# A SwiGLU down projection: where the third tile's sums are loaded, when the last norm's vectors are loaded, and the order of the weight loads

## The chip, the cores and the metric

The kernel runs on one core of a Trainium2 chip. The metric is the device time of one execution, in microseconds; lower is better. A change counts as faster or slower here from two per cent on.

## What is computed

One decoder block over 256 tokens of width 1024: two token mixers with a shared input projection, an output projection, a layer norm, and a SwiGLU feed-forward layer with 2816 hidden features and a second layer norm. The change is in the last lines, the down projection and the norm behind it:

```python
D_MODEL = 1024
SEQ = 256
D_FF = 2816

def layer_norm(x, w, b):
    mu = jnp.mean(xf, axis=-1, keepdims=True)
    var = jnp.mean(jnp.square(xf - mu), axis=-1, keepdims=True)
    y = (xf - mu) * lax.rsqrt(var + LN_EPS) * w + b
    ...

    x = layer_norm(DN_ALPHA * x + mixed, ln1_w, ln1_b)
    h = jnp.einsum('bsd,df->bsf', x, w_ffn_in)
    h_gate, h_up = jnp.split(h, 2, axis=-1)
    y = jnp.einsum('bsf,fd->bsd', jax.nn.silu(h_gate) * h_up, w_ffn_down)
    return layer_norm(DN_ALPHA * x + y, ln2_w, ln2_b)
```

## The kernel before

**Precision.** Every float32 operand is split in two float32r parts: ScalarE casts it to the high part, VectorE subtracts to get the low part. TensorE then makes three products for one (high by high, high by low, low by high). A weight tile therefore goes through a load, a cast on ScalarE and a subtraction on VectorE before TensorE can use it.

**The down projection.** The 2816 rows of the down weights are 11 tiles of 256 rows by 1024 columns. Eight of them are *fast* tiles: their 2 x 2 blocks are multiplied by a Strassen-Winograd scheme with seven block products instead of eight, so 21 matmuls of 512 columns a tile. Three of the weight blocks are blocks of the tile itself (the *corners*), four are sums of blocks (the *sums*). The activations' sums are made when the hidden features come out (lines 1017 to 1022). The other three tiles are *plain* (`rows_pass`). `SEQUENCE` takes the fast tiles first, then the plain ones. In the built program the weights are numbered through the whole kernel: the fast tiles are 66 (first) to 73 (eighth), so 68 is the third and 69 the fourth, and the plain ones are 74 to 76.

**Where the sums come from.** `DOWN = "STTSTTSTPPP"` says it by tile. In an S tile (first, fourth, seventh) VectorE makes the sums from the corners' raw weights, in two places of 1024 columns, `cst` and `mv1` (lines 246 to 250); in a T tile (second, third, fifth, sixth, eighth) they were made much earlier, during the up projection, by DMAs that add in DRAM (`sum_weights`), and are loaded from there like a weight (line 271).

**Places.** Raw weights are loaded into `wraw` (3 places of 1 MB, one place is freed by the subtraction on VectorE of the tile that holds it) or into `big` (12 places of 1 MB, which activations, the residual and the norms' vectors use as well). `whi` and `wlo`, 4 places each, hold the high and low parts; a place is free again when TensorE has made its last product with it. Before the change the corners of the fourth to eighth tile go to `big` (line 254) and all loaded sums to `wraw`. The last norm's vectors `wb2`, 2 x 512 KB broadcast over the partitions by GpSimd's queue, take a place of `big` ahead of the down projection (line 1030).

**Order.** PE, DVE and Activation run in the order of the code in this part (`manual_schedule`). SyncE's loads are put in order by the scheduler. A queue is in order: a load whose place is not free holds those behind it.

Of the kernel before, what the change touches and what calls it, by code (L numbers as in the profile page):

```python
# [10 lines left out]
F32 = mybir.dt.float32  # L11
# [6 lines left out]
P = 128  # L18
T = 256
NT = T // P  # L20
D = 1024
# [24 lines left out]
FAST = tuple(range(2, 2 + len(DOWN) - DOWN.count("P")))  # L46
PLAIN = tuple(q for q in range(NF // 2) if q not in FAST)
SEQUENCE = [PLAIN[DOWN[:i].count("P")] if s == "P" else FAST[i - DOWN[:i].count("P")] for i, s in enumerate(DOWN)]
SUMMED = [q for q, s in zip(SEQUENCE, DOWN) if s == "T"]

C_ID = 0
# [32 lines left out]
def plan():  # L84
# [3 lines left out]
    def add(w, k0, kn, c0, n, held=False):  # L88
        tiles.append((w, k0, kn, c0 if isinstance(c0, tuple) else (c0,), n, held))
# [29 lines left out]
    for j in range(EARLY, NF, 2):  # L119
        add("w_ffn_in", 0, 8, j * P, 256)  # L120
        add("w_ffn_in", 0, 8, FF + j * P, 256)
    for q in SEQUENCE:
        add("w_ffn_down", 2 * q, 2, 0, 1024)
# [4 lines left out]
def hybrid_layer_kernel(ctx: ExitStack, tc, x, xw, vecs, bias, wts, ln1_w, ln1_b, ln2_w, ln2_b, consts, out):  # L128
    nc = tc.nc
    pool = lambda name, bufs, **kw: ctx.enter_context(tc.tile_pool(name=name, bufs=bufs, **kw))  # L130
    cp = pool("cp", 1)
# [9 lines left out]
    def slot(name, dt=F32):  # L141
        return big.tile([P, 2048], dt, tag="s8", name=name)

    def r32(ap):
        return ap.bitcast(F32)
# [32 lines left out]
    down = {t[1] // 2: i for i, t in enumerate(tiles) if t[0] == "w_ffn_down"}  # L178
# [6 lines left out]
    corners = {}  # L185
    dram = pool("dram", 1, space=bass.MemoryType.DRAM)
    summed = {down[q]: dram.tile([P, 2048], F32, tag=f"sums{q}", name=f"sums{q}") for q in SUMMED}
    state = {"next": 0}
# [9 lines left out]
    def stage(pieces=None, eng=nc.vector):  # L198
# [18 lines left out]
        for ks in ks_of(pieces or (k,)):  # L217
            nc.sync.dma_start(raw[:, ks, :], src[:, ks, :])
            if i in SUMS_AFTER and ks.start == 0:
                sum_weights(down[SUMMED[SUMS_AFTER.index(i)]])  # L220
            nc.scalar.copy(h[:, ks, :], raw[:, ks, :])  # L221
# [5 lines left out]
    quarters = lambda z: z.rearrange("p (b c) -> p b c", b=4)  # L227
# [13 lines left out]
    def stage_fast(i, kind):  # L241


        def make_sums(b):
            y, z = corners[i] = [v.rearrange("p (b c) -> p b c", b=2) for v in (
                cst, cp.tile([P, D], F32, tag="mv1", name=f"sums{i}"))]
            nc.vector.tensor_add(y, b[:, 1:3, :], b[:, 0:1, :].to_broadcast([P, 2, 512]))
            yield
            nc.vector.tensor_add(z[:, 0, :], b[:, 2, :], y[:, 0, :])
            nc.vector.tensor_add(z[:, 1, :], b[:, 3, :], z[:, 0, :])  # L250

        beside = kind == "corners" and i not in [down[q] for q in SEQUENCE[0:3]]
        raw = lambda: quarters(slot(f"raw{kind}{i}") if beside else
                               wraw.tile([P, 2048], F32, tag="raw", name=f"raw{kind}{i}"))
        h = quarters(whi.tile([P, 2048], F32R, tag="h", name=f"wh{kind}{i}"))
        l = quarters(wlo.tile([P, 2048], F32R, tag="l", name=f"wl{kind}{i}"))
        if kind == "corners":
            b = raw()
            n = 1 if i in summed else 0
            nc.sync.dma_start(b[:, n:4, :], quarters(wts[i])[:, n:4, :])  # L260
            sums = make_sums(b) if n == 0 else iter(())
            next(sums, None)
            h, l = h[:, 0:3, :], l[:, 0:3, :]
            nc.scalar.copy(h, b[:, 1:4, :])  # L264
            yield
            list(sums)
            nc.vector.tensor_sub(l, b[:, 1:4, :], r32(h))  # L267
            yield
        elif i in summed:
            z = raw()  # L270
            nc.sync.dma_start(z, quarters(summed[i]))
            nc.scalar.copy(h, z)  # L272
            yield
            nc.vector.tensor_sub(l, z, r32(h))  # L274
            yield
        else:
            for z, bs in zip(corners.pop(i), (slice(0, 2), slice(2, 4))):
                nc.scalar.copy(h[:, bs, :], z)
                yield
                nc.vector.tensor_sub(l[:, bs, :], z, r32(h[:, bs, :]))  # L280
                yield
        ready.append((h, l))
# [14 lines left out]
    cst = cp.tile([P, C_MASK], F32, tag="cst", name="cst")  # L297
# [165 lines left out]
    for j in range(4):  # L463
        sg = sm.tile([P, 2, T], F32, tag="sg", name=f"sgq{j}")
        sgs = [by_half(sg[:, f, :]) for f in range(2)]
        if j < HQ_WIDE:
            for f, ps in enumerate(wide_pair(f"hq{j}", xp, mm, "mm")):
                z = Qg[:, :, 2 * j + f, :]
# [7 lines left out]
        for f in range(2):  # L476
            h = 2 * j + f
# [213 lines left out]
    mv1 = cp.tile([P, D], F32, tag="mv1", name="mv1")  # L691
# [151 lines left out]
    def bcast(name, w, b):  # L843
        t = slot(name).rearrange("p (a d) -> p a d", a=2)
        nc.gpsimd.dma_start(t[:, 0, :], w[0].partition_broadcast(P))
        nc.gpsimd.dma_start(t[:, 1, :], b[0].partition_broadcast(P))
        return t
# [179 lines left out]
    with tc.manual_schedule(engines={ET.PE, ET.DVE, ET.Activation}):  # L1027
        for j in range(NF - 2 * ORDERED, NF, 2):
            last_gate = ffn_step(j)
        wb2 = bcast("wb2", ln2_w, ln2_b)  # L1030
        bank = lambda p, n: p.tile([P, 512], F32, tag="aux" if p is aux else "mm", name=n)
        p2, p4, p1, p5 = [bank(mm, f"wp{i}") for i in (2, 4, 1, 5)]
        p7, p3, wd0, p6 = [bank(aux, f"wp{i}") for i in (7, 3, 0, 6)]
# [3 lines left out]
        ends = dict(ktot=2 * PLAIN[-1] + 2)  # L1037
        begins = {id(ps): SEQUENCE[0] for ps in (p2, p3, p4)}
        begins.update({id(wd0): PLAIN[0]})
# [13 lines left out]
        def into_residual():  # L1053
            u = slot("u").rearrange("p (b c) -> p b c", b=4)
            first, second = slice(0, 512), slice(512, D)
            res = lambda t, ns, z: nc.vector.scalar_tensor_tensor(x1[:, t, ns], x1[:, t, ns], ALPHA, z,
                                                                  op0=ALU.mult, op1=ALU.add)
            nc.scalar.copy(u[:, 0, :], p1)
            res(1, second, p1)
            nc.vector.tensor_add(u[:, 1, :], p6, u[:, 0, :])  # L1060
            nc.vector.tensor_add(u[:, 2, :], p7, u[:, 1, :])
            nc.vector.tensor_sub(u[:, 3, :], p5, u[:, 1, :])
            res(1, first, u[:, 3, :])
            res(0, second, u[:, 2, :])
            nc.vector.tensor_sub(u[:, 0, :], p5, u[:, 2, :])
            res(0, first, u[:, 0, :])

        held = []
        for i, q in enumerate(SEQUENCE):
            if q in FAST:  # L1070
                fast(q)
                if q == FAST[0]:
                    split(act_plain[PLAIN[-1]][:, 0], act_plain[PLAIN[-1]][:, 1], last_gate)
                if q == FAST[-1]:
                    into_residual()
                continue
            tile_q = [(2 * q,) + fetch()]
            if i < len(SEQUENCE) - HOLD_DOWN:
                for part in late:
                    rows_pass([part], lhs, 1, tile_q, first=2 * begins[id(part[0])], **ends)  # L1080
            else:
                held += tile_q
            for part in early:
                rows_pass([part], lhs, 0, tile_q, first=2 * begins[id(part[0])], **ends)
        y = slot("y").rearrange("p (t d) -> p t d", t=NT)
        z, spare = [slot("z")[:, i:i + D] for i in (0, D)]
# [7 lines left out]
        sums = sm.tile([P, 2 * HOLD_DOWN], F32, tag="bst", name="wsum")  # L1094
        for i, (raw, (k0, wh, wl)) in enumerate(zip(last_raw, held)):
# [5 lines left out]
            c = sums[:, 2 * i:2 * i + 2].unsqueeze(2).to_broadcast([P, 2, SUMS])  # L1101
# [106 lines left out]
```

## Time and profile before

| | us |
|---|---|
| median of 3 runs | 492.29 |
| the runs | 491.97, 492.29, 1702.07 |
| the profiled execution, its own time | 492.29 |
| its span, first to last instruction | 490.5 |

The first run of the three, 1702.07 us, is a single outlier and is left out of what follows; the profiled execution is the median one, and 1.79 us of its time lie outside the span. Over the span TensorE is busy 478.2 us (97%), VectorE 387.7 (79%), ScalarE 293.5 (60%), GpSimd 57.6 (12%).

In the rows of the profile a tile's name stands without its number: `whcorners` and `wlcorners` are the high and low parts of the corners, `whsums` and `wlsums` those of the sums, `rawcorners` and `rawsums` the loaded weights, `cst` and `sums` the places of VectorE's own sums, `wp` the accumulators of the down projection, `fu` and `fg` the up projection ahead of it. A timeline row has the start in us, the duration, the engine, the source line, the operation, output and inputs, and in brackets the idle time ahead of it with what ended it. PE is TensorE, DVE is VectorE, ACT is ScalarE, POOL is GpSimd, SPq is SyncE's DMA queue. A row of a DMA issue ends with its size and the microseconds from issue to landing. Line numbers are those of the kernel before.

### The profile page before, as it was taken

The page shows a single profiled execution, that of the slowest core. Times are in us where ns is not written, and L with a number is a line of the kernel's source. Part 1 is how long each engine was busy: PE and PEld are TensorE (multiplying, and loading weights), DVE is VectorE, ACT ScalarE, POOL GpSimd, SP SyncE. Part 2 cuts the span into 40 slices and gives each one's busy share as a digit, 9 for nine tenths or more (in the row PEclk, how much of TensorE's full clock was granted, in tenths as well). Part 3 has the DMA queues.
Part 4 walks back from the last instruction along what each step waited for, and adds up shares of the span by engine and source line. Part 5 has one row for each costly group of instructions (what it writes and reads, how often), then busy time and mean ns, then how long its engine had stood idle before and what let it go on. Part 6 is the DMA issues. An engine that isn't in the chain of part 4 may idle for free.

```text
span 490.5 us, 7432 instructions
## 1 busy us (share of the span) xinstructions
PE 478.2 (97%) x2956; PEld 409.4 (83%) x2956; DVE 387.7 (79%) x503; ACT 293.5 (60%) x407; POOL 57.6 (12%) x62
## 2 busy tenths in 40 slices
PE   9999999999999999999999999999999999979993
PEld 8888888788899888888888888888888888857883
DVE  4889895899948889998465688656886779859976
ACT  6698665538565787667733453455566554646662
POOL 0000000000024522322101000102110000000120
PEclk9999999999999999999999999999999999999998
DMA  8986537522842454268889762899998744498442
GB/s 308 418 304 253 172 144 284 216 87 98 321 184 93 155 206 171 108 255 293 253 276 269 210 246 86 258 286 264 324 207 310 238 150 152 160 425 307 169 118 86
DMA packets 21667, 108.70 MB, mean 222 GB/s; under 512 B 2432, under 2 KB 4224, under 8 KB 11904
## 3 DMA queue, kind: packets, MB, share of 16 engines
q1 hardware_dynamic: 16128, 98.13, 54.4%
q0 software_dynamic: 5360, 9.96, 10.5%
q8 instruction: 23, 0.38, 0.3%
q10 hardware_dynamic: 144, 0.13, 0.1%
q14 instruction: 12, 0.10, 0.1%
HBM read 105.59 MB, written 11.53 MB: 239 GB/s over the span
## 4 chain that ended last, share of the span: by engine, by line
PE 82%; DVE 9%; DMA 3%; issue 2%; ACT 2%; DVEq 0%; POOLq 0%; POOL 0%; ACTq 0%
PE fg L342 6%; PE fu L342 5%; PE fg L344 3%; PE hq L342 3%; PE fu L344 3%; PE mq L342 2%; PE mk L342 2%; DMA rawsums<-sums 2%; DVE wlcorners L267 2%; PE mv L393 2%; PE gb L393 2%; PE hg L393 2%; PE hf L367 2%; PE hq L344 2%; PE ga L393 1%
## 5 line engine op out<-in xcount | busy, mean ns | idle before, releaser
L223 DVE TENSOR_TENSOR wl<-raw,wh 128x2048 fp32r<-128x2048 f32 (+1 forms) x70 | 160.3, 2294 | 56.7 <-ACT wh L221 56.1
L221 ACT CAST wh<-raw 128x2048 fp32r<-128x2048 f32 (+1 forms) x70 | 131.5, 1887 | 60.6 <-PE fg L342 14.0
L342 PE MATMUL fg<-x1p,wh 128*128 128x512 f32 x144 | 50.5, 394 | 0.0
L342 PE MATMUL fu<-x1p,wh 128*128 128x512 f32 x144 | 50.4, 394 | 0.0
L344 PE MATMUL fg<-x1p,wl 128*128 128x256 f32 x144 | 40.0, 278 | 0.0
L344 PE MATMUL fu<-x1p,wl 128*128 128x256 f32 x144 | 39.9, 277 | 0.0
L342 PEld LDWEIGHTS fu<-x1p,wh 128*128 128x128 f32 x144 | 27.0, 187 | 6.2
L342 PEld LDWEIGHTS fg<-x1p,wh 128*128 128x128 f32 x144 | 27.0, 187 | 6.1
L344 PEld LDWEIGHTS fg<-x1p,wl 128*128 128x128 f32 x144 | 27.1, 188 | 0.1
L344 PEld LDWEIGHTS fu<-x1p,wl 128*128 128x128 f32 x144 | 27.1, 188 | 0.0
L745 POOL TENSOR_TENSOR rtk<-rtk,cst 128x512 f32<-128x512 f32 x4 | 6.2, 1556 | 163.6 <-ACT rtk L743 163.6
L342 PE MATMUL hq<-xp,wh 128*128 128x512 f32 x64 | 22.2, 394 | 0.0
L344 PE MATMUL hq<-xp,wl 128*128 128x256 f32 x64 | 17.7, 277 | 0.0
L342 PE MATMUL mq<-xp,wh 128*128 128x512 f32 x48 | 17.0, 398 | 0.0
L342 PE MATMUL mk<-xp,wh 128*128 128x512 f32 x48 | 16.7, 395 | 0.0
L274 DVE TENSOR_TENSOR wlsums<-rawsums,whsums 128x2048 fp32r<-128x2048 f32 x5 | 11.4, 2287 | 5.4 <-ACT whsums L272 5.4
L235 POOL DMA_DIRECT2D sums<-sums x10 | 8.1, 811 | 64.4 <-DMA sums<-sums 33.0
L267 DVE TENSOR_TENSOR wlcorners<-rawcorners,whcorners 128x1536 fp32r<-128x1536 f32 x8 | 14.0, 1752 | 2.1 <-ACT whcorners L264 2.1
L342 PEld LDWEIGHTS hq<-xp,wh 128*128 128x128 f32 x64 | 12.0, 188 | 2.8
L272 ACT CAST whsums<-rawsums 128x2048 fp32r<-128x2048 f32 x5 | 9.6, 1912 | 7.4 <-DMA rawsums<-sums 6.2
L235 POOL DMA_DIRECT2D sums<-in_wts_dram x10 | 8.4, 988 | 42.5 <-DMA sums<-in_wts_dram 42.5
L344 PE MATMUL mq<-xp,wl 128*128 128x256 f32 x48 | 13.2, 281 | 0.0
(371 smaller groups left out, 1343.3 us busy)
## 6 DMA issues: line engine op xcount, KB each, us to landing
raw<-in_wts_dram SPq DMA_DIRECT2D x68, 1024.0 KB, 4.8
sums<-in_wts_dram SPq DMA_DIRECT2D x10, 512.0 KB, 8.5
rawsums<-sums SPq DMA_DIRECT2D x5, 1024.0 KB, 8.2
xw<-in_xw_dram SPq DMA_DIRECT2D x6, 640.0 KB, 9.1
rawcorners<-in_wts_dram SPq DMA_DIRECT2D x5, 768.0 KB, 8.3
rawcorners<-in_wts_dram SPq DMA_DIRECT2D x3, 1024.0 KB, 7.7
sums<-in_wts_dram POOLq DMA_DIRECT2D x10, 256.0 KB, 8.5
sums<-sums POOLq DMA_DIRECT2D x10, 256.0 KB, 6.7
```

Source lines behind the costliest of these rows:

```text
L221: nc.scalar.copy(h[:, ks, :], raw[:, ks, :])
L223: eng.tensor_sub(l[:, ks, :], raw[:, ks, :], r32(h[:, ks, :]))
L235: more = lambda dst, src: nc.gpsimd.dma_start(dst, src, accum_op=ALU.add)
L267: nc.vector.tensor_sub(l, b[:, 1:4, :], r32(h))
L272: nc.scalar.copy(h, z)
L274: nc.vector.tensor_sub(l, z, r32(h))
L342: nc.tensor.matmul(ps, wh[:, k, wcol], a.both(k), start=(k == 0), stop=False)
L344: nc.tensor.matmul(ps[:, 0, :], wl[:, k, wcol], a[0, k, slice(0, T)], start=False, stop=(k == KC - 1))
L367: nc.tensor.matmul(ps, wh[:, kk, wcol], xp.both(k), start=False, stop=False)
L393: nc.tensor.matmul(pss[t], ah[:, kk, ts], wh[:, k, :], start=(kk == 0), stop=False)
L745: nc.gpsimd.tensor_mul(tmp, tmp, bc(sin))
```

## The change

Four edits in the staging of the fast tiles, and one move:

- the sums of the third tile are loaded in two halves of 512 KB into the two places in which VectorE had the first tile's sums (`cst` and `mv1`), and cast and subtracted in two halves; `cst` becomes a tile of its own for each use;
- a table, `BESIDE`, says which raw weights go to `big`: the corners of the fourth, seventh and eighth tile and the sums of the fifth and eighth; the corners of the fifth and sixth now go to `wraw`;
- these loads stay in the order of the code (`keep_in_program_order`);
- `wb2` is loaded behind the eighth fast tile in the code, so that it takes another place of `big`.

```diff
+BESIDE = ((3, "corners"), (4, "sums"), (6, "corners"), (7, "corners"), (7, "sums"))
...
         def make_sums(b):
             y, z = corners[i] = [v.rearrange("p (b c) -> p b c", b=2) for v in (
-                cst, cp.tile([P, D], F32, tag="mv1", name=f"sums{i}"))]
+                [cp.tile([P, D], F32, tag=tag, name=f"sums{tag}{i}") for tag in ("cst", "mv1")])]
...
-        beside = kind == "corners" and i not in [down[q] for q in SEQUENCE[0:3]]
-        raw = lambda: quarters(slot(f"raw{kind}{i}") if beside else
+        at = SEQUENCE.index(next(q for q in FAST if down[q] == i))
+        raw = lambda: quarters(slot(f"raw{kind}{i}") if (at, kind) in BESIDE else
                                wraw.tile([P, 2048], F32, tag="raw", name=f"raw{kind}{i}"))
+        load = lambda dst, src: tc.keep_in_program_order(nc.sync.dma_start(dst, src))
...
-            nc.sync.dma_start(b[:, n:4, :], quarters(wts[i])[:, n:4, :])
+            load(b[:, n:4, :], quarters(wts[i])[:, n:4, :])
...
         elif i in summed:
-            z = raw()
-            nc.sync.dma_start(z, quarters(summed[i]))
-            nc.scalar.copy(h, z)
+            if at == 2:
+                parts = [(z.rearrange("p (b c) -> p b c", b=2), slice(2 * n, 2 * n + 2)) for n, z in enumerate(
+                    (cp.tile([P, D], F32, tag="cst", name=f"raw0{i}"), cp.tile([P, D], F32, tag="mv1", name=f"raw1{i}")))]
+            else:
+                parts = [(raw(), slice(0, 4))]
+            for z, bs in parts:
+                load(z, quarters(summed[i])[:, bs, :])
+            for z, bs in parts:
+                nc.scalar.copy(h[:, bs, :], z)
             yield
-            nc.vector.tensor_sub(l, z, r32(h))
+            for z, bs in parts:
+                nc.vector.tensor_sub(l[:, bs, :], z, r32(h[:, bs, :]))
             yield
...
             last_gate = ffn_step(j)
-        wb2 = bcast("wb2", ln2_w, ln2_b)
...
                 if q == FAST[-1]:
+                    wb2 = bcast("wb2", ln2_w, ln2_b)
                     into_residual()
```

SyncE's queue from the third tile's corners to the first plain tile, before. The number behind `rawcorners` or `rawsums` is the tile's:

```order
L260 DMA rawcorners68_3982<-in_wts_dram 128x1536
L260 DMA rawcorners69_4017<-in_wts_dram 128x2048
L271 DMA rawsums68_4002<-sums4_85 128x2048
L271 DMA rawsums70_4072<-sums6_86 128x2048
L271 DMA rawsums71_4105<-sums7_87 128x2048
L260 DMA rawcorners70_4054<-in_wts_dram 128x1536
L260 DMA rawcorners71_4087<-in_wts_dram 128x1536
L271 DMA rawsums73_4175<-sums9_88 128x2048
L260 DMA rawcorners72_4120<-in_wts_dram 128x2048
L260 DMA rawcorners73_4157<-in_wts_dram 128x1536
L218 DMA raw74_4188<-in_wts_dram 128x2048
```

The same part of the queue now, with the third tile's two halves as `raw068` and `raw168`:

```order
L256 DMA rawcorners68_3980<-in_wts_dram 128x1536
L256 DMA raw068_4000<-sums4_85 128x1024
L256 DMA raw168_4001<-sums4_85 128x1024
L256 DMA rawcorners69_4019<-in_wts_dram 128x2048
L256 DMA rawcorners70_4057<-in_wts_dram 128x1536
L256 DMA rawsums70_4075<-sums6_86 128x2048
L256 DMA rawcorners71_4090<-in_wts_dram 128x1536
L256 DMA rawsums71_4108<-sums7_87 128x2048
L256 DMA rawcorners72_4123<-in_wts_dram 128x2048
L256 DMA rawcorners73_4161<-in_wts_dram 128x1536
L256 DMA rawsums73_4179<-sums9_88 128x2048
L219 DMA raw74_4192<-in_wts_dram 128x2048
```

The third tile's sums moved ahead of the fourth tile's corners, and each tile's corners now stand ahead of its sums and of the next tile.

VectorE from the third tile's corners to those of the fourth, before (`ap1` is a part of the activations, `room` a hidden feature tile):

```order
L267 TENSOR_TENSOR wlcorners68_3981<-rawcorners68_3982,whcorners68_3980 128x1536
L192 TENSOR_TENSOR ap1_2624<-room_3056,ap1_2624 128x512
L274 TENSOR_TENSOR wlsums68_4001<-rawsums68_4002,whsums68_4000 128x2048
L247 TENSOR_TENSOR cst_92<-rawcorners69_4017 128x1024
L249 TENSOR_TENSOR sums69_4019<-rawcorners69_4017,cst_92 128x512
L250 TENSOR_TENSOR sums69_4019<-rawcorners69_4017,sums69_4019 128x512
L267 TENSOR_TENSOR wlcorners69_4016<-rawcorners69_4017,whcorners69_4015 128x1536
```

And now:

```order
L269 TENSOR_TENSOR wlcorners68_3979<-rawcorners68_3980,whcorners68_3978 128x1536
L193 TENSOR_TENSOR ap1_2624<-room_3056,ap1_2624 128x512
L283 TENSOR_TENSOR wlsums68_3999<-raw068_4000,whsums68_3998 128x1024
L283 TENSOR_TENSOR wlsums68_3999<-raw168_4001,whsums68_3998 128x1024
L248 TENSOR_TENSOR sumscst69_4021<-rawcorners69_4019 128x1024
L250 TENSOR_TENSOR sumsmv169_4022<-rawcorners69_4019,sumscst69_4021 128x512
L251 TENSOR_TENSOR sumsmv169_4022<-rawcorners69_4019,sumsmv169_4022 128x512
L269 TENSOR_TENSOR wlcorners69_4018<-rawcorners69_4019,whcorners69_4017 128x1536
```

Nothing else moves on VectorE: the one subtraction became two, and the fourth tile's first sum is written over what the first of them reads. ScalarE's row is changed in the same way, one cast into two, and TensorE's row has the same instructions in the same order. On GpSimd `wb2` is still ahead of the copies `eh` and `el` of the last plain tiles' parts; it now waits for the place of the fourth tile's corners.

## The prediction

> **What bounds the kernel now.** I read the page first, then the busy time by stretches, then the timelines of the engines around the one stretch that is not full. Columns of the second view: stretch, its length, then busy time of each engine with its instruction count, granted clock, DMA share, GB/s.
>
> ```profile
> span 490.5 us, 7432 instructions
> ...
> core 0: us, PE busy (x) PEld busy (x) DVE busy (x) ACT busy (x) POOL busy (x), PEclk, DMA share, GB/s
> 422.00:434.00 12.00, 12.00 (x56) 9.98 (x55) 7.60 (x7) 5.17 (x7) 1.07 (x2) 1.00 0.89 334
> 434.00:443.00 9.00, 5.24 (x21) 3.45 (x20) 7.79 (x7) 6.47 (x6) 0.00 (x0) 1.00 1.02 421
> 443.00:466.00 23.00, 23.00 (x101) 18.71 (x100) 22.93 (x15) 15.10 (x10) 1.84 (x3) 1.00 0.62 227
> ```
>
> TensorE is full on both sides of 434 to 443 and short by 3.8 us within it, while the DMA engines are full at 421 GB/s. The clock granted is 1.00 throughout, so this is waiting. Its price on TensorE shows in the matmul starts: the first product of the eight fast tiles, the last product of the first tile and of the second, the last before the gap, the first behind it, and the first of the plain tiles.
>
> ```profile
> 422.72 0.39 PE L1049 MATMUL wp<-whcorners,ash 128*128 128x512 f32 x1
> ...
> 427.28 0.39 PE L1051 MATMUL wp<-whsums,asl 128*128 128x512 f32 x1
> ...
> 432.04 0.39 PE L1051 MATMUL wp<-whsums,as 128*128 128x512 f32 x1
> ...
> 434.08 0.39 PE L1051 MATMUL wp<-whcorners,as 128*128 128x512 f32 x1
> 435.17 0.51 PE L1049 MATMUL wp<-whsums,as 128*128 128x512 f32 x1 [0.70 <-ACT whsums L272]
> ...
> 465.81 0.39 PE L859 MATMUL wp<-wh,ap 128*128 128x512 f32 x1
> ```
>
> A fast tile is 21 products and takes 432.04 - 427.28 = 4.76 us (0.227 us a product) with its operands there. Six more would end with the next product starting at 432.04 + 6 x 4.76 + 0.23 = 460.83. It starts at 465.81, so TensorE loses 4.98 us. What it waits for stands in the chain of waits:
>
> ```profile
> 423.85 9.26 DMA rawsums<-sums
> 433.20 1.92 ACT whsums L272
> 435.14 2.29 DVE wlsums L274
> ...
> 462.13 4.78 DMA raw<-in_wts_dram
> ```
>
> The third tile's sums are asked for at 423.85 and land 9.3 us later; ScalarE and VectorE then split them, and VectorE runs without a pause up to the last plain tile, whose load in turn is issued only at 462.13. The two waits of VectorE, and the places that the change uses, in its timeline (ScalarE's last row ahead of its wait is first):
>
> ```profile
> 426.38 0.62 ACT L191 CAST ap<-room 128x512 fp32r<-128x512 f32 x1
> ...
> 416.98 1.22 DVE L280 TENSOR_TENSOR wlsums<-cst,whsums 128x1024 fp32r<-128x1024 f32 x1
> 418.11 1.22 DVE L280 TENSOR_TENSOR wlsums<-sums,whsums 128x1024 fp32r<-128x1024 f32 x1
> ...
> 429.01 0.69 DVE L192 TENSOR_TENSOR ap<-room,ap 128x512 fp32r<-128x512 f32 x1
> 435.14 2.29 DVE L274 TENSOR_TENSOR wlsums<-rawsums,whsums 128x2048 fp32r<-128x2048 f32 x1 [5.45 <-ACT whsums L272]
> 437.35 1.22 DVE L247 TENSOR_TENSOR cst<-rawcorners 128x1024 f32<-128x1024 f32 x1
> ...
> 439.94 1.75 DVE L267 TENSOR_TENSOR wlcorners<-rawcorners,whcorners 128x1536 fp32r<-128x1536 f32 x1
> ...
> 442.75 1.22 DVE L280 TENSOR_TENSOR wlsums<-sums,whsums 128x1024 fp32r<-128x1024 f32 x1
> ...
> 468.96 2.29 DVE L223 TENSOR_TENSOR wl<-raw,wh 128x2048 fp32r<-128x2048 f32 x1 [2.45 <-ACT wh L221]
> ```
>
> **The change, part by part.** Sizes and microseconds to landing of single loads, alone and in the full stretch, with what holds SyncE's queue for the fourth tile's corners and when GpSimd issues wb2 behind the same matmuls:
>
> ```profile
> SPq L260 <- PE fu L344: 11.0, 1, 11.0
> 421.94 0.59 POOL L845 DMA_DIRECT2D wb<-in_ln_w_dram  x1 [44.47 <-PE fu L344]
> raw<-in_wts_dram SPq DMA_DIRECT2D x1, 1024.0 KB, 4.8
> rawcorners<-in_wts_dram SPq DMA_DIRECT2D x1, 768.0 KB, 4.1
> rawcorners<-in_wts_dram SPq DMA_DIRECT2D x1, 1024.0 KB, 7.7
> rawcorners<-in_wts_dram SPq DMA_DIRECT2D x1, 768.0 KB, 10.9
> wb<-in_ln_b_dram POOLq DMA_DIRECT2D x1, 512.0 KB, 7.1
> eh<-wh POOLq DMA_DIRECT2D x1, 256.0 KB, 2.6
> ```
>
> *Third tile's sums in two halves.* Their places come free when VectorE has read the first tile's sums: 416.98 + 1.22 = 418.20 and 418.11 + 1.22 = 419.33, instead of 423.85. No 512 KB load of that queue is shown alone; its bounds are the 2.6 us of 256 KB and, with the engines full, 10.9 us. I take 3.5 us, a step of 0.6 to 0.7 below the 4.1 of 768 KB and the 4.8 of a megabyte, since nothing else is moving then: 421.7 and 422.9; at 10.9 us the second half would be 1.6 us late. ScalarE may cast them only when TensorE has left the place they are cast into, which the first tile's sums hold until 427.28 + 0.39 = 427.67; ScalarE's row at 426.38 is over by 427.0. So it casts at 427.7 and 428.7, and up to 5 us more in the loads would cost nothing. VectorE follows at 429.01 + 0.61 = 429.62 (rows follow each other at some 0.08 less than their length) with two halves at 1.13 each, and reaches the fourth tile's first sum at 431.88 instead of 437.35: 5.47 us earlier. The extra instruction on each engine costs 0.05 to 0.1 us, counted there.
>
> *Order of the loads, wb2.* The fourth tile's corners take the place in the big pool that wb2 took, free by 421.94 at the latest. With 4.8 to 7.7 us they land at 426.7 to 429.6; ScalarE needs them at 429.7, VectorE at 431.88. I take 427, as wb2's megabyte no longer shares the engines; at 10.9 us they would be 1.0 us late. Everything behind in the queue is issued earlier than before or at the same time: the fourth to eighth tile need 7.6 MB, 18 us at 421 GB/s, done near 442 while ScalarE comes to the last of them at 451, and each of them lands some 5 us or more ahead of its turn. SyncE waits at the halves until 419.3, but TensorE uses the place of the next load until about 421.9 anyway. The plain tiles' loads follow the fifth and sixth tile's splits and the last one is out near 446 instead of 462.13, so VectorE's second wait of 2.45 us goes too. wb2 is issued when the fourth tile's corners are split, 439.94 - 5.47 + 1.75 = 436.2; with 7.1 us, or 10.9, it is there by 447, and wanted at 470.8 (below).
>
> *Where TensorE would wait next.* It starts the fourth tile at 432.04 + 0.23 + 4.76 = 437.0 and its sums 9 products later at 439.1. VectorE has the corners at 436.2 and the sums at 442.75 - 5.47 + 1.22 = 438.5: margins of 0.8 and 0.6 us, the smallest of all eight tiles (later ones 0.8 to 2). So TensorE loses none of its 4.98 us.
>
> **The end.** Here TensorE's last two groups meet the norm's chain:
>
> ```profile
> 480.38 0.28 PE L861 MATMUL wp<-eh,ap 128*128 128x258 f32 x1
> 482.53 0.28 PE L861 MATMUL more<-wh,ap 128*128 128x256 f32 x1
> 478.68 1.42 DVE L1110 SCALAR_TENSOR_TENSOR z<-y,n2sum,wb 128x512 f32<-128x512 f32 x2
> 482.07 0.21 DVE L1158 TENSOR_SCALAR n2sum<-wp,n2sum 128x1 f32<-128x1 f32 x1
> 483.72 0.46 ACT L1113 ACTIVATE z<-more,n2sum 128x256 f32<-128x256 f32 x1
> 484.08 0.20 ACT L1113 ACTIVATION_READ_ACCUMULATOR z<-more,n2sum 128x1 f32 x1
> 484.52 0.16 DVE L1168 TENSOR_TENSOR n2sum<-n2sum 128x1 f32<-128x1 f32 x1
> ```
>
> VectorE's chain is 5.47 + 2.45 = 7.9 us earlier, TensorE 4.98: TensorE now arrives last. Its last product ends at 482.81 - 4.98 = 477.83, ScalarE squares it from 477.85 to 478.41 (0.56, as from 483.72 to 484.28), and L1168 starts at 478.44 instead of 484.52: 6.08 us earlier. Of this, 4.98 is TensorE's gap and 1.1 the slack that the chain before had behind TensorE. What follows is unchanged. Sum: 490.5 - 6.1 = 484.4 us of span; the profiled execution took 492.29, 1.79 around its span, and is itself the median. So 486.2 us.
>
> [...] The 4.98 us stands only if 0.227 us a product is TensorE's own pace. It does where VectorE is ahead: the sixth tile's sums are split by
>
> ```profile
> 449.42 2.28 DVE L274 TENSOR_TENSOR wlsums<-rawsums,whsums 128x2048 fp32r<-128x2048 f32 x1
> ```
>
> 451.7, and first used at 465.81 - 2 x 4.76 - 12 x 0.227 = 453.6, so TensorE has work in store and still takes 4.76 us a tile. [...]
>
> **Rivals.**
> 1. *Loads still late.* The fourth tile's corners land 14 us after 421.94, at 436: VectorE 4 us late, TensorE 4 - 0.8 = 3.2 us, 489.4 us. Against it: no load here took longer than 10.9 us, and that one had a queue ahead of it.
> 2. *A new wait at the fourth tile.* Its corners and sums cost VectorE more than 4.76 us, the margins are 0.6 to 0.8. If a hand-over that I put at 0.03 to 0.08 us takes 1 to 2 us in all, TensorE waits that less the margin: 486.6 to 487.6.
> 3. *VectorE's gain counts whole.* If TensorE could go faster than 0.227, the end moves by 7.9 us: 484.4. [...]
> 4. *Nothing moves.* Some other release holds the third tile's sums to 433: 492.3. Against it: the places are read last from 418.11 on, and GpSimd, which adds up the sums in DRAM, had been idle for 44 us by 421.94.
> 5. *Slower: wb2 late.* It is now issued while VectorE has no pause until 463. VectorE wants it at 478.68 - 7.9 = 470.8 and has 7.9 - 6.1 = 1.8 us to spare there; the gain is gone when it lands 6.1 after that, at 478.7, 42 us after its issue, and each later microsecond is one over 492.3: 494.6 for a landing at 481. Against it: GpSimd's eh copy, issued at 460.67 with VectorE full, landed in 2.6 us. [...]
>
> **How the numbers follow.** Forecast 0.75, rivals in order 0.08, 0.07, 0.04, 0.03, 0.03. The predicted time is the forecast's, 486.2. The range goes down to 485.3 (the spread of the two lowest times, 0.3, and half of the 1.1 us slack misjudged) and up to 489.4, rival 1's time; outside are rivals 3, 4 and 5, 0.10, and some of rival 1. Two per cent, 9.8 us, is about what a measurement of this kernel can tell from no change: the forecast's 1.2% is within it, and so are rivals 1 to 4 and most of 5. I leave 0.02 to faster, out of rival 3's share (it has no floor shown), 0.02 to slower, out of rival 5's, 0.96 to within.
>
> **What would show it.** Right: VectorE's idle of 5.45 us ahead of the third tile's sums is under 0.3; TensorE full from 422 to the plain tiles, which start near 460.8; the last plain load issued near 446; the fourth tile's corners landing before 429.7; L1168 released by ScalarE's square at about 478.4. Wrong: an idle of TensorE at the fourth tile (rival 1 if ScalarE waits for the DMA ahead of it, rival 2 if not), a product pace other than 0.227, or VectorE waiting for wb2.

## The result and the profile after

| | before | after |
|---|---|---|
| median, us | 492.29 | 485.71 |
| the runs, us | 491.97 to 492.42, once 1702.07 | 485.54 to 486.00 (5 runs) |
| ratio of after to before | | 0.9868, 95% interval 0.9853 to 0.9884 |
| span of the profiled execution, us | 490.5 | 484.0 |
| its own time, us | 492.29 | 485.77 |

The change takes 6.6 us off, 1.3%. That is within the two per cent that count as no change here, but the interval lies clear of 1. Three single executions, of three kernels, stand far off (1702.07, 802.77 and 684.08 us); the comparisons leave them out.

The page of the profile gives the shares of the chain that ended last, the work followed back from the last instruction. Before:

```profile
PE 82%; DVE 9%; DMA 3%; issue 2%; ACT 2%; DVEq 0%; POOLq 0%; POOL 0%; ACTq 0%
```

After, with the span:

```profile
span 484.0 us, 7438 instructions
...
PE 96%; issue 1%; DMA 1%; ACT 1%; DVE 0%; DVEq 0%; POOLq 0%; POOL 0%; SPq 0%
```

TensorE now carries the chain up to 470.6 us, where the rows of the last norm begin. The only load left in it is the first of the kernel, 3.70 us at 1.18, and VectorE's share, 9% before, is 0%. The busy time by stretches, with the same columns as before:

```profile
422.00:434.00 12.00, 12.00 (x56) 9.94 (x55) 11.90 (x12) 8.64 (x9) 0.00 (x0) 1.00 1.00 374
434.00:443.00 9.00, 9.00 (x42) 7.44 (x41) 9.00 (x7) 7.13 (x6) 1.14 (x2) 1.00 1.01 420
443.00:466.00 23.00, 23.00 (x103) 19.00 (x102) 22.79 (x18) 18.50 (x25) 5.54 (x9) 1.00 0.66 231
```

The middle stretch was short of 3.8 us on TensorE and is full; VectorE works 11.90 instead of 7.60 us in the first stretch, because it no longer waits there. The same starts of products as before: the first one of the eight fast tiles, the last ones of the first tile, and the first of the plain tiles.

```profile
422.57 0.39 PE L1057 MATMUL wp<-whcorners,ash 128*128 128x512 f32 x1
...
427.13 0.39 PE L1059 MATMUL wp<-whsums,asl 128*128 128x512 f32 x1
...
460.77 0.39 PE L868 MATMUL wp<-wh,ap 128*128 128x512 f32 x1
```

From the first fast product to the first plain one TensorE takes 460.77 - 422.57 = 38.20 us; before it was 465.81 - 422.72 = 43.09. So 4.89 us of the gain are TensorE's gap. This length, first fast product to first plain product, is the measure used for every run below: what it has over 38.20 is what TensorE lost at the eight fast tiles.

VectorE at the same place, and its last rows that wait:

```profile
428.87 0.69 DVE L193 TENSOR_TENSOR ap<-room,ap 128x512 fp32r<-128x512 f32 x1
429.47 2.35 DVE L283 TENSOR_TENSOR wlsums<-raw,whsums 128x1024 fp32r<-128x1024 f32 x2
431.74 1.22 DVE L248 TENSOR_TENSOR sumscst<-rawcorners 128x1024 f32<-128x1024 f32 x1
...
456.41 6.68 DVE L224 TENSOR_TENSOR wl<-raw,wh 128x2048 fp32r<-128x2048 f32 x3
...
473.22 0.21 DVE L1158 TENSOR_SCALAR n2sum<-n2sum 128x1 f32<-128x1 f32 x1 [1.02 <-ACT z L1122]
...
475.62 0.22 DVE L1167 TENSOR_SCALAR n2sum<-wp,n2sum 128x1 f32<-128x1 f32 x1 [0.58 <-PE wp L870]
...
478.37 0.16 DVE L1177 TENSOR_TENSOR n2sum<-n2sum 128x1 f32<-128x1 f32 x1 [0.39 <-ACT z L1122]
```

Both of VectorE's waits are gone (no bracket at L283, none at the three plain tiles of L224), and pauses have come in behind 473 instead: VectorE now waits for TensorE at the end, directly or through ScalarE. From the last product on, TensorE's last row to the end of the span, there were 490.5 - 482.53 = 7.97 us before and are 484.0 - 477.45 = 6.55 now:

```profile
477.45 0.28 PE L870 MATMUL more<-wh,ap 128*128 128x256 f32 x1
```

The 6.5 us of span are thus 4.89 at the fast tiles, 1.42 behind the last product, and 0.15 by which the down projection already starts earlier, with a rest of 0.04 in the products between.

### The profile page after: what moved, and what is told of

The parts are those of the page before. It is cut to its first block, busy times and chain, and to the rows that moved or that the text cites. A ratio compares the mean times of both kernels' runs of the same rounds, so it can differ in the third digit from the quotient of the medians.

```text
span 484.0 us, 7438 instructions
## 1 busy us (share of the span) xinstructions
PE 476.5 (98%) x2956; PEld 409.0 (85%) x2956; DVE 387.8 (80%) x504; ACT 294.1 (61%) x408; POOL 58.2 (12%) x62
## 4 chain that ended last, share of the span: by engine, by line
PE 96%; issue 1%; DMA 1%; ACT 1%; DVE 0%; DVEq 0%; POOLq 0%; POOL 0%; SPq 0%
PE fu L351 7%; PE fg L351 7%; PE fg L353 3%; PE fu L353 3%; PE hq L351 3%; PE wp L1059 3%; PE wp L1058 3%; PE wp L1057 3%; PE mq L351 2%; PE mk L351 2%; PE gb L402 2%; PE mv L402 2%; PE hg L402 2%; PE hq L353 2%; PE hf L376 2%; PE mv L404 2%
## 5 line engine op out<-in xcount | busy, mean ns | idle before, releaser
L224 DVE TENSOR_TENSOR wl<-raw,wh 128x2048 fp32r<-128x2048 f32 (+1 forms) x70 | 160.2, 2294 | 53.8 <-ACT wh L222 53.5
L353 PE MATMUL mk<-xp,wl 128*128 128x256 f32 x48 | 12.8, 277 | 0.0
L402 PE MATMUL mv<-wh,xp 128*128 128x512 f32 x32 | 12.7, 398 | 0.0
```

The lines of the kernel that those rows point to most:

```text
L224: eng.tensor_sub(l[:, ks, :], raw[:, ks, :], r32(h[:, ks, :]))
L353: nc.tensor.matmul(ps[:, 0, :], wl[:, k, wcol], a[0, k, slice(0, T)], start=False, stop=(k == KC - 1))
L402: nc.tensor.matmul(pss[t], ah[:, kk, ts], wh[:, k, :], start=(kk == 0), stop=False)
```

## The experiments

Two questions. Which of the parts brings the gain: the halves, the late `wb2`, the written order, the new places? And is it TensorE that sets the time now, as the prediction has it, and with how much in hand on VectorE?

The changed kernel was also run once more as a yardstick for the runs beside it.

> The changed kernel once more, as the yardstick for the runs beside it: 485.5 to 486.1 us, TensorE without a gap from 420 to 478.

Its runs took 485.45 to 486.09 us, ratio 0.9868 (0.9852 to 0.9885): the same as the first time. That TensorE has no gap is shown for the first time only; no profile of these runs shows it.

All runs in one table. A mark says which part of the change a kernel has; "lost" is TensorE's length from the first fast to the first plain product over 38.20; "behind" is the span's end less the start of TensorE's last product. Both are of the profiled execution; the ratio is to the runs of the kernel before that were made beside each kernel, so rows are best compared by it.

| kernel | halves | wb2 late | order | places | lost, us | behind, us | median, us | ratio to before, 95% |
|---|---|---|---|---|---|---|---|---|
| before | | | | | 4.89 | 7.97 | 492.29 | 1 |
| wb2 alone | | x | | | 2.62 | 8.06 | 491.31 | 0.9977 (0.9966 to 0.9987) |
| places alone | | | | x | 5.03 | 6.92 | 491.02 | 0.9975 (0.9965 to 0.9985) |
| halves alone | x | | | | 4.23 | 7.84 | 491.17 | 0.9977 (0.9967 to 0.9987) |
| halves and order | x | | x | | 0.00 | 7.69 | 487.22 | 0.9901 (0.9884 to 0.9917) |
| halves and wb2 | x | x | | | 0.00 | 7.66 | 486.76 | 0.9890 (0.9875 to 0.9904) |
| sums whole | | x | x | x | 0.41 | 6.96 | 486.78 | 0.9885 (0.9868 to 0.9901) |
| wb2 early | x | | x | x | 0.00 | 6.89 | 486.02 | 0.9872 (0.9857 to 0.9887) |
| free order | x | x | | x | 0.00 | 6.50 | 485.76 | 0.9869 (0.9854 to 0.9884) |
| after | x | x | x | x | 0.00 | 6.55 | 485.71 | 0.9868 (0.9853 to 0.9884) |

**The halves alone.** The kernel before with the two halves in `cst` and `mv1` (with `cst` as a tile for each use), and nothing else:

```diff
-            z = raw()
-            nc.sync.dma_start(z, quarters(summed[i]))
...
+            if i == down[SEQUENCE[2]]:
+                parts = [(z.rearrange("p (b c) -> p b c", b=2), slice(2 * n, 2 * n + 2)) for n, z in enumerate(
+                    (cp.tile([P, D], F32, tag="cst", name=f"raw0{i}"), cp.tile([P, D], F32, tag="mv1", name=f"raw1{i}")))]
+            else:
+                parts = [(raw(), slice(0, 4))]
+            for z, bs in parts:
+                nc.sync.dma_start(z, quarters(summed[i])[:, bs, :])
```

> The kernel before with the third tile's sums in two halves in the places of VectorE's sums and nothing else changed: wb2 early, the other loads as before. Theory (the halves alone bring TensorE's whole 4.98 us, and VectorE's second wait stays): TensorE has no gap over 0.5 us from 422 to 460; VectorE is 5.47 us earlier at the fourth tile and still waits about 2.4 us for the last plain tile, so that its chain, 1.1 us behind TensorE before, sets the end together with it: 5.5 us off, near 486.8. Rival (the other two parts were needed): the fourth tile's corners, issued near 422.9 beside wb2, land at 433 or later, TensorE loses 2 us or more there, 488 or more.

Neither came true as described. The third and the fourth tile run without a gap, but TensorE loses 4.23 us behind them, most of it at the fifth tile, where the rival did not look. The rival's 488 or more is met, by another load than the one it named: the fourth tile's corners land at 430.8, not at 433. SyncE's issues and the rows of ScalarE and TensorE at the fifth tile:

```profile
422.82 0.33 SPq L260 DMA_DIRECT2D rawcorners<-in_wts_dram  x1
423.75 5.61 SPq L276 DMA_DIRECT2D rawsums<-sums  x3
429.69 0.33 SPq L260 DMA_DIRECT2D rawcorners<-in_wts_dram  x1
...
441.49 1.47 ACT L264 CAST whcorners<-rawcorners 128x1536 fp32r<-128x1536 f32 x1 [5.93 <-DMA rawcorners<-in_wts_dram]
...
443.01 0.50 PE L1056 MATMUL wp<-whcorners,as 128*128 128x512 f32 x1 [1.15 <-ACT whcorners L264]
444.81 0.50 PE L1057 MATMUL wp<-wlcorners,as 128*128 128x512 f32 x1 [1.29 <-DVE wlcorners L267]
...
rawcorners<-in_wts_dram SPq DMA_DIRECT2D x1, 768.0 KB, 11.7
```

The three `rawsums` issued from 423.75 on are those of the fifth, sixth and eighth tile, three megabytes; behind them, at 429.69, come the fifth tile's corners, 768 KB, which land only 11.7 us later, at 441.4. ScalarE was ready for them 5.93 us before. So the halves remove one late load and uncover another, which before had the third tile's 5 us of delay as its cover: there it landed at 440.0 and was cast at 441.0 without a wait. The time gained is about 1 us of 6.6, 491.17 against a median of 492.16 for the kernel before beside it.

**Halves and order; halves and wb2.** Two ways to get the fifth tile's corners out from behind the sums. The first adds the written order to the kernel with the halves alone; the second, instead, moves `wb2` behind the eighth tile, so that the place it leaves takes a corner load early.

```diff
+        load = lambda dst, src: tc.keep_in_program_order(nc.sync.dma_start(dst, src))
...
-            nc.sync.dma_start(b[:, n:4, :], quarters(wts[i])[:, n:4, :])
+            load(b[:, n:4, :], quarters(wts[i])[:, n:4, :])
...
-                nc.sync.dma_start(z, quarters(summed[i])[:, bs, :])
+                load(z, quarters(summed[i])[:, bs, :])
```

> The kernel before with the halves and the written order of the loads; old places, wb2 early. Theory (with the halves alone the fifth tile's corners were late through the three megabytes of sums issued ahead of them): these corners are issued near 429.7 us with nothing but the fourth tile's corners in flight and land by 436, so no gap of TensorE over 0.6 us; VectorE's wait for the last plain tile stays at some 2.4 us and its chain sets the end: 485.9 to 486.9. Rival (the place that is freed at 429.7 is what made them late): they land at 438 or later, TensorE loses over 1.5 us, 487.5 or more.

```diff
-        wb2 = bcast("wb2", ln2_w, ln2_b)
...
                 if q == FAST[-1]:
+                    wb2 = bcast("wb2", ln2_w, ln2_b)
                     into_residual()
```

> The kernel before with the halves and wb2's loads behind the eighth fast tile; old places by the old rule, no order held. The place that wb2 leaves lets the fifth tile's corners be issued near 422.9 us, ahead of the sums of the fifth, sixth and eighth tile; the sixth tile's corners come behind them, near 429.7. Theory (the late load is whichever stands behind three megabytes of sums): the fifth tile's corners land by 432 and cost nothing; the sixth tile's land near 441, wanted by ScalarE at 441 and by VectorE at 442.2, TensorE loses under 0.6 us; VectorE's wait for the last plain tile stays: 485.9 to 487.0. Rival (the order held is needed): TensorE loses over 1.5 us at the fifth or sixth tile, 487.5 or more.

Both theories held: TensorE loses nothing in either. With the order, the corners are issued at the same 429.7 as with the halves alone, into the same place, and land in 4.4 us instead of 11.7:

```profile
rawcorners<-in_wts_dram SPq DMA_DIRECT2D x1, 768.0 KB, 4.4
```

The load that was late was late through what stood ahead of it. Most of what both still lack to the changed kernel, 1.0 to 1.5 us, lies behind the last product: 7.7 us instead of 6.5 in the profiled executions. VectorE still waits for the last plain tile, here in the kernel with halves and order, and its chain comes to the end last, with no pause left at the lines where the changed kernel waits for TensorE:

```profile
463.67 2.29 DVE L223 TENSOR_TENSOR wl<-raw,wh 128x2048 fp32r<-128x2048 f32 x1 [2.49 <-ACT wh L221]
```

The median with the order, 487.22, lies 0.3 above the range given.

**The sums whole.** The changed kernel without the halves:

```diff
-            if at == 2:
+            if False:
```

> The changed kernel with the third tile's sums loaded whole into a place of the raw pool, as before; wb2 late and the loads in written order, so that these sums are issued ahead of the fourth tile's corners, near 423.8. Theory (the halves' gain is their early place): with 5 to 7.7 us they land at 429 to 431.5, ScalarE casts 2 us behind that, VectorE is 1.6 to 4 us behind the changed kernel, TensorE has 0.56 us of margin and loses 1 to 3.5: 486.7 to 489.2. Rival (written order and a late wb2 are enough by themselves): no idle of VectorE over 0.5 us, 485.5 to 486.2.

The time, 486.78, is at the lower end of the theory's and above the rival's, but not by the theory's mechanism. The sums are issued at 423.8, as in the kernel before, and land in 4.8 us (before: 9.3); VectorE idles 0.95 us, which the fourth tile's margin takes up to 0.41.

```profile
430.57 2.29 DVE L283 TENSOR_TENSOR wlsums<-rawsums,whsums 128x2048 fp32r<-128x2048 f32 x1 [0.95 <-ACT whsums L280]
...
rawsums<-sums SPq DMA_DIRECT2D x1, 1024.0 KB, 4.8
```

So the late place was not the cause that the theory took it for: with the same place and the same issue time, 4.5 of the 4.9 us come back when nothing is issued ahead of this load. Here both the order and the late `wb2` clear the way. The order with the sums whole and `wb2` early was not run, so what it would bring without the others is open.

**wb2 alone; places alone.** The kernel before with one part each: `wb2`'s line moved as in the diff above, and the table `BESIDE` in place of the old rule (with `cst` as a tile for each use):

```diff
-        beside = kind == "corners" and i not in [down[q] for q in SEQUENCE[0:3]]
-        raw = lambda: quarters(slot(f"raw{kind}{i}") if beside else
+        at = SEQUENCE.index(next(q for q in FAST if down[q] == i))
+        raw = lambda: quarters(slot(f"raw{kind}{i}") if (at, kind) in BESIDE else
```

> The kernel before with wb2's two loads behind the eighth fast tile and nothing else changed: the third tile's sums keep their megabyte place in the raw pool. Theory (the place, freed late, holds those sums; the megabyte of wb2 beside them is a minor matter): the sums are still issued near 423.8 us, now behind the fourth and fifth tile's corners, and land near 432 to 433; VectorE's idle ahead of them stays 4 to 5.5 us, TensorE's gap 4 to 5 us, the time 491.5 to 492.5. Rival (the bandwidth that wb2 takes is what makes them late): a megabyte less in the engines, at 421 GB/s 2.5 us, so they land near 430.6, TensorE's gap is about 2.5 us and the time near 490.

> The kernel before with only the five loads of the new table put beside the raw pool: third tile's sums whole, wb2 early, no order held. The third tile's sums are then issued near 423.8 us behind the fourth tile's corners and wb2, as before. Theory (those sums are late through what is in flight ahead of them, whatever the later loads' places): they land near 433, TensorE's gap of 4 to 5 us stays; the last plain tile is no longer awaited by VectorE, which takes the 1.1 us slack behind TensorE: 491.0 to 492.2. Rival (the new places by themselves bring the gain, as nothing else was missing in the run with whole sums): 487.5 or less.

With `wb2` moved, the sums are issued at 423.60, behind 1 MB and 768 KB of corners that went out from 421.27 on, and land in 7.0 us, at 430.6, where the rival had them; TensorE loses 2.62.

```profile
rawsums<-sums SPq DMA_DIRECT2D x1, 1024.0 KB, 7.0
```

That profiled execution, 489.91, was the fastest of its kernel; the others took 490.50 to 491.86, so mostly less came of it, and the median, 491.31, lies between the two forecasts, 0.85 us under that of the kernel before beside it, 492.16. The 7.0 and the 2.62 are thus of one favourable execution. With the places alone the sums land after 9.4 us, TensorE loses its 5 us as the theory had it, and only the end gains. Its VectorE row, to be held against the 5.45 of before, and its load:

```profile
434.80 2.29 DVE L283 TENSOR_TENSOR wlsums<-rawsums,whsums 128x2048 fp32r<-128x2048 f32 x1 [5.55 <-ACT whsums L280]
...
rawsums<-sums SPq DMA_DIRECT2D x1, 1024.0 KB, 9.4
```

What the places bring at the end shows in the whole table when "behind" is counted only up to the start of VectorE's last `n2sum` row (L1168 before, L1177 after, its like in the others). That is 0.91 to 0.92 us in all five profiled kernels of the table with the new places, this one among them, and 1.73 to 2.07 in the five without. So the slack behind TensorE goes with the places, whatever else a kernel has. The rest, from that row to the end of the span, varies from 5.58 to 6.05 us between the profiles with the same instructions in it, so differences of 0.4 in "behind" say nothing.

The landings of the third tile's sums now stand in a row, for a megabyte issued between 423.4 and 423.9 in each kernel: 4.8 us with nothing issued in the 2 us ahead (sums whole); 7.0 with 1.75 MB of corners, of which the first megabyte is 2.3 us old (wb2 alone); 9.3 and 9.4 with the fourth tile's corners and `wb2`, 2 MB within 2 us ahead (before, places alone). At the 421 GB/s of the full stretch a megabyte takes 2.5 us, and 4.8 + 2 x 2.5 = 9.8 would be the estimate for the last two, which were measured at 9.3 and 9.4.

**wb2 early; free order.** The changed kernel with `wb2` back at its old line, and the changed kernel with plain issues in `load`:

```diff
+        wb2 = bcast("wb2", ln2_w, ln2_b)
         bank = lambda p, n: p.tile([P, 512], F32, tag="aux" if p is aux else "mm", name=n)
...
                 if q == FAST[-1]:
-                    wb2 = bcast("wb2", ln2_w, ln2_b)
                     into_residual()
```

```diff
-        load = lambda dst, src: tc.keep_in_program_order(nc.sync.dma_start(dst, src))
+        load = lambda dst, src: nc.sync.dma_start(dst, src)
```

> The changed kernel with wb2 loaded ahead of the down projection, as before; the halves and the written order of the loads stay. Theory (the halves carry the gain, wb2's place does not): the fourth tile's corners are issued near 422.9 instead of 421.4 and share the engines with wb2's megabyte, but land by 429.7; later loads are later and still ahead of their turn; TensorE has no gap over 0.3 us and the time is 485.5 to 486.3. Rival (moving wb2 was needed to keep the fourth tile's corners in time): they land at 433 or later, ScalarE is 3 us late with them, TensorE loses about 2 us or more, 487.5 to 489.5.

> The changed kernel without the order held as written: the new places, the halves and the late wb2 stay, and only the fifth tile's corners and the sixth tile's sums change places in SyncE's queue. Theory (the places and the halves already give this order nearly, so holding it is worth nothing): the fifth tile's corners come a megabyte later, near 432.5, wanted at about 434.9 or later: no gap, 485.5 to 486.2. Rival (the written order carries part of the gain, as the fifth tile's corners were late where the halves stood alone): they land at 438 or later, TensorE loses 1.5 to 3 us, 487.3 to 489.

Both theories held in the time and in TensorE's gap, and neither part is needed once the others are there: nothing lost on TensorE, 486.02 and 485.76. One step of the first was missed: with `wb2` early the fourth tile's corners land 8.1 us after 422.52, at 430.6 and not by 429.7. That is 1.35 us later than ScalarE could have taken them, and VectorE does not wait:

```profile
430.72 1.48 ACT L266 CAST whcorners<-rawcorners 128x1536 fp32r<-128x1536 f32 x1 [1.35 <-DMA rawcorners<-in_wts_dram]
```

**What sets the time now.** Two more VectorE instructions ahead of the fourth tile, and seven products fewer on TensorE:

```diff
-            for z, bs in parts:
+            for z, bs in parts * (2 if at == 2 else 1):
                 nc.vector.tensor_sub(l[:, bs, :], z, r32(h[:, bs, :]))
```

> The changed kernel with VectorE's two halves of the third tile's sums done twice over, so two instructions of 1024 columns more, 2.26 us, ahead of the fourth tile. Theory (TensorE sets the pace and VectorE has 0.56 us in hand at the fourth tile's sums, 0.79 at its corners): TensorE loses 2.26 - 0.56 = 1.7 us there and none elsewhere, VectorE's 2 us of pauses at the end take up its own delay: 487.4. Rival A (VectorE sets the pace to the end): the whole 2.26 us, 488.0. Rival B (the margin is larger than the rows show): under 1 us.

```diff
-                    nc.tensor.matmul(ps, ah[:, a, :], wl[:, b, :], start=False, stop=False)
+                    if q != FAST[-1]:
+                        nc.tensor.matmul(ps, ah[:, a, :], wl[:, b, :], start=False, stop=False)
```

> The changed kernel without the seven products of the high parts with the weights' low parts in the eighth fast tile; its weights' low parts are still made. Theory (TensorE sets the end, at 0.227 us a product): its plain tiles start 7 x 0.227 = 1.59 us earlier, its last product ends near 476.1, VectorE's pauses of 1.02, 0.58 and 0.39 us at the end shrink by that in all, and the time is 1.3 to 1.6 us lower, 484.1 to 484.4. Rival (VectorE's chain or the loads set the end and TensorE only keeps step): under 0.4 us, 485.3 or more.

With the two instructions TensorE's length at the fast tiles is 462.48 - 422.61 = 39.87, so 1.67 us lost of VectorE's 2.26, all of it at the fourth tile; the time is 487.55, ratio 0.9905 (0.9888 to 0.9921). The time alone doesn't exclude rival A's 488.0. The profile does: 0.6 of the 2.26 never reached TensorE, the next waits at the end are still for TensorE, and what lies behind the last product is the same 6.54 us.

The rows: the fourth tile's first sum, 2.3 us later than in the changed kernel, TensorE's first wait, and VectorE's last.

```profile
434.06 1.21 DVE L248 TENSOR_TENSOR sumscst<-rawcorners 128x1024 f32<-128x1024 f32 x1
...
438.44 0.50 PE L1058 MATMUL wp<-wlcorners,as 128*128 128x512 f32 x1 [1.14 <-DVE wlcorners L269]
...
480.07 0.16 DVE L1177 TENSOR_TENSOR n2sum<-n2sum 128x1 f32<-128x1 f32 x1 [0.39 <-ACT z L1122]
```

Without the seven products the length is 458.92 - 422.31 = 36.61, 1.59 us under 38.20 and so exactly 7 x 0.227, and the time is 484.29, ratio 0.9838 (0.9823 to 0.9853), 1.4 us under the changed kernel's. The seven products that went took their 0.227 us each off TensorE's row, and the end followed; TensorE sets the time. VectorE's pauses at the end shrink from 1.02, 0.58 and 0.39 to 0.31, none and 0.39, so there is little left beyond that.

```profile
458.92 0.39 PE L868 MATMUL wp<-wh,ap 128*128 128x512 f32 x1
...
472.06 0.21 DVE L1159 TENSOR_SCALAR n2sum<-n2sum 128x1 f32<-128x1 f32 x1 [0.31 <-ACT z L1123]
...
476.52 0.16 DVE L1178 TENSOR_TENSOR n2sum<-n2sum 128x1 f32<-128x1 f32 x1 [0.39 <-ACT z L1123]
```

## Why the prediction was right, and where it was not

**The sum was right.** 486.2 was predicted and 485.71 measured. Its terms against the trace: TensorE's gap 4.98, measured 4.89; the slack behind TensorE 1.1, measured 1.07 (L1168 started 1.71 us after the last product's end, L1177 starts 0.64 after it). The rest of 0.5 us is in two terms that were not there: the down projection starts 0.15 earlier, and from L1177 to the end of the span it is 5.63 us instead of 5.98, with the same instructions. That second term is no part of the mechanism: the last stores land 2.0 us after their issue in both, so the difference lies behind them, and the kernels above have 5.58 to 6.05 there (halves and `wb2` 5.64, sums whole 6.05). What sets it no run shows. The prediction also took two per cent as about what a measurement here can tell from no change; the interval, 0.9853 to 0.9884, is a third of a per cent wide.

**The halves.** Issued at 418.18 and 419.21, as worked out. Their landing was mis-sized: 3.5 us were taken, 4.2 and 5.8 measured, so 422.4 and 425.0. As the prediction said, up to 5 us more cost nothing, since ScalarE can cast only at 427.60 (427.7 predicted); VectorE splits them at 429.47 and starts the fourth tile at 431.74 (429.62 and 431.88).

```profile
raw<-sums SPq DMA_DIRECT2D x1, 512.0 KB, 4.2
raw<-sums SPq DMA_DIRECT2D x1, 512.0 KB, 5.8
```

**The fourth tile's corners, the later loads, wb2.** The corners land at 421.37 + 6.2 = 427.6 (427 taken; 436 in rival 1), 2 us ahead of their cast. The claim that all later loads land some 5 us or more ahead of their turn was a little too good: the leads are 3.6 us (the seventh tile's corners, 10.6 us after 429.63) to 6.5. The last plain load is out at 446.1 (446). `wb2` is issued at 436.53 and lands by 447.9 (436.2 and 447), 22.8 us before its first use at 470.71: rival 5, `wb2` there too late, is refuted. Its two loads took 7.6 and 10.8 us with 420 GB/s moving in all and VectorE busy for 11.34 of the 11.37 us from 436.53 to 447.90, so they were not held up for long.

**TensorE's margins.** 0.8 and 0.6 us were read from the trace of before; after, they are 436.87 + 0.23 - (434.33 + 1.75) = 1.0 us at the first low-part product of the fourth tile's corners, and 439.14 - 438.35 = 0.8 at that of its sums, counted to the product that reads the low part rather than to the one before it. That they are as small as worked out is shown by the 2.26 us put ahead of them, of which 1.67 came through. Rival 2 did not happen. The pace of 0.227 us a product, which the prediction took as TensorE's own, held over the 168 products of the eight fast tiles (38.20 us, at a granted clock of 1.00) and in the run with seven products fewer (36.61 us for 161); so rival 3 is out as well.

**The step that failed** is the share-out, not the sum. The prediction put the whole 4.98 us down to the halves' earlier place ("their places come free when VectorE has read the first tile's sums ... instead of 423.85") and took the order and `wb2` only as what keeps the later loads in time, with no share of the gain. It did not ask why the load before had taken 9.3 us. The runs show that half of those 9.3 us were other loads in the queues ahead (4.8 us with nothing issued in the 2 us before), that the sums in their old place are nearly on time when they go first (0.41 lost), and that the halves without the other parts are worth about 1 us, since the fifth tile's corners are then late in the same way. The sentence "everything behind in the queue is issued earlier than before or at the same time" is true of the whole change, and it is the order of the loads that makes it so, or else the place that `wb2` leaves; either will do. The second term of the sum, the 1.1 us of slack, is the places' share, as the prediction's step on the plain tiles' loads has it.

**Not foreseen.** ScalarE's squares for the first rows stand behind copies that wait for TensorE (L1141, 5.21 us), and that is where VectorE's pause of 1.02 us at L1158 comes from. It costs nothing, as TensorE arrives last anyway.

```profile
470.62 0.38 ACT L1141 COPY wp<-y 128x256 f32<-128x256 f32 x1 [5.21 <-PE wp L1139]
```

## What to carry to other kernels

Where a load lands late, look first at how much was issued ahead of it in the microseconds before: while the DMA engines were full (a share of 1.00 from 423.85 to 433.10 before), the landing of the third tile's sums, 9.3 and 9.4 us, was about its own time and that of what had just been issued in front, estimated above at 9.8, and a clear way for the load (the order with the late `wb2`) was nearly as good a remedy as an earlier place: 0.41 us lost on TensorE against none. A wait that is taken away can uncover the next late load, here two tiles further, so follow each later load to its own use before counting a gain, and ask of each part of a change what it brings without the others. When one engine has become the only chain, its start-to-start length between two fixed instructions is a sharper measure than the total time: here it told 0.4 us from nothing, where the times overlapped.

## What was not expected of the hardware

In the kernel with the places alone TensorE's granted clock fell for some 3.4 us after the gap, and its products came every 0.42 to 0.43 us from 437.54 to 440.53 instead of every 0.23. The stretches, with the clock in the third number from the end:

```profile
434.00:437.00 3.00, 0.51 (x2) 0.19 (x1) 2.20 (x1) 2.14 (x2) 0.00 (x0) 1.00 1.02 427
437.00:439.00 2.00, 1.85 (x5) 1.47 (x6) 1.93 (x4) 0.66 (x1) 0.00 (x0) 0.60 1.02 430
439.00:441.00 2.00, 2.00 (x7) 1.57 (x6) 2.00 (x2) 1.67 (x3) 0.00 (x0) 0.54 1.00 422
441.00:444.00 3.00, 3.00 (x14) 2.26 (x13) 3.00 (x4) 3.00 (x3) 0.00 (x0) 1.00 0.98 350
```

In the profiled execution of the kernel before, the same gap left the clock at 1.00. The mean granted clocks of the runs suggest that this goes either way: 3.4 us at half clock are 0.0035 of 489 us, and the two profiled executions have 0.993 and 0.997. Of the 38 runs of the kernel before beside the experiments 23 have 0.990 to 0.993 and 15 have 0.996 or 0.997, while the eight runs of the changed kernel in the two comparisons, which has no gap, have 0.996 or more. Where in those runs the clock was low is not recorded.

What set the clock down stays open. With the places alone only one product starts between 433.63 and 437.15, at 434.82; in the kernel before, whose clock stayed at 1.00, it is one between 434.08 and 437.49 as well, at 435.17.

It cost little here. From 437.15 to 440.90 nine products took 3.75 us, 1.7 more than at 0.227 each. Yet TensorE loses 5.03 us with the slow spell and 4.89 without it, because the kernel before waits again for VectorE at the fourth tile, which the kernel with the places alone does not:

```profile
441.75 0.50 PE L1050 MATMUL wp<-wlcorners,as 128*128 128x512 f32 x1 [1.23 <-DVE wlcorners L267]
```

The 23 runs with the low mean have a median of 492.14 us, the 15 others 492.40. Where no such wait follows, these nine products would put the cost of a slow spell at 1.7 us on top of the gap's own length: an estimate, which no run here shows.
